# The head of a hybrid encoder block: GpSimd's first low parts behind VectorE's copies, and the first unit's products ordered by pass

## The chip, the cores and the metric

The kernel runs on one core of a Trainium2 chip. The metric is the device time of one execution in microseconds, lower is better. The core's engines are TensorE (PE; its weight loads are shown as PEld), VectorE (DVE), ScalarE (ACT), GpSimd (POOL) and SyncE (SP), which here only issues transfers.

## The reference

The block takes x (1 x 256 x 1024, float32) and computes

- h = RMSNorm(x), with a gain per channel, and z = h @ W_in, 8192 columns: pool input and gate, q, k, v of three groups of eight heads, attention gate, merge-gate logits;
- branch A: centred means over windows of 2, 4, 8 and 16 minus the token, a map per group, times SiLU of the gate, projected to 1024;
- branch B: attention in three groups with windows and strides (128,1), (512,4), (2048,16), each with a relative-position bias from a table of 32 buckets, merged by the softmax denominators, gated, projected to 1024;
- merge = sigmoid(gA) * yA + sigmoid(gB) * yB; x + merge @ W_out; a last RMSNorm.

All of it is float32. The changed part is the beginning: the first norm, its transposed output, and the first k columns of z:

```
def _rmsnorm(x, g):
    xf = x.astype(jnp.float32)
    r = lax.rsqrt(jnp.mean(xf * xf, axis=-1, keepdims=True) + RMS_EPS)
    return (xf * r).astype(x.dtype) * g
...
        h = _rmsnorm(x, norm_gain[l])
        z = h @ w_in[l]
```

## The kernel before, in words

**Split products.** Every float32 matrix product is made of three products of a rounded format (`F32R`). Each operand is cut into a high part, the value rounded to that format, and a low part, the rest: `whi` and `wlo` for weights, `hh` and `hl` for the normed activations. One 128x128 block of a product costs three matmuls (high by high, low by high, high by low), summed in PSUM (`mm3`, L253 to L256).

**Units of weights.** The weights stream in as units of 1 MB (a unit of W_in: 8 blocks of 128 rows, `kc` 0 to 7, by 256 columns; `load_next` issues one from SyncE, L101). Four raw buffers `wraw`, three pairs `whi`, `wlo`. Unit n is cut in halves of four `kc` by `cut_half` (L117): ScalarE writes `whi` (L128), VectorE subtracts and writes `wlo` (L133). TensorE uses each unit for two blocks of 128 columns, 24 matmuls each. The results leave PSUM through ScalarE and VectorE: three PSUM tiles of the tag `mm` take turns for them. Units 0, 1, 2 are the k columns of the three head groups; q and v follow, then the rest.

**Who sets the order.** In the head (L172 to L250) the order is written by hand: `tc.manual_schedule` keeps the order of the code for ScalarE, VectorE, TensorE and GpSimd. After it a scheduler orders the instructions of each engine from its own costs. SyncE's transfers stand in the order in which they are written. Each engine runs its instructions in order and waits on semaphores.

**The head.** Transfers go out in this order: x in two blocks of 128 rows, unit 0 in two halves, unit 1, the bias table `oh` (L147), unit 2, unit 3. ScalarE issues the parameters `prm` (L78), which hold among others the norm gain. Then:

1. TensorE runs twelve products of a zero tile (`keep_warm`, L179) that nothing reads.
2. For each of the two blocks of x, ScalarE and VectorE each square and sum one half (L185, L187), VectorE adds the two (L190), GpSimd raises the sum to -0.5 (L191). Then VectorE scales the first half of the columns (L194) and ScalarE the second (L195) into `XN`.
3. For unit 0 the cut is different: VectorE copies both halves of `wraw` to `whi` (L197) and GpSimd subtracts for `wlo` (L163), one half each after the copy of that half.
4. TensorE transposes the eight column blocks of the first block of x (L202), runs two products of the zero tile, transposes those of the second, runs one more. Four PSUM tiles `tp` take them, two column blocks each.
5. For each `kc`, ScalarE writes `hh` from PSUM times the gain (L228), and VectorE writes `hl` (L229), the rest. The fifth to eighth `hh` wait for the `hl` that reads the same PSUM tile.
6. TensorE multiplies unit 0 (`part0`, L207): for each `kc` two matmuls with `hh` (L212) and, right behind them, two with `hl` (L217); for the first four `kc` those with `wlo` follow after the sixth high one (L214), for the last four at the end. Then come three small products that look up the bias lines (L245); VectorE copies them out between the cuts of units 1 and 2 (L248).

After the head TensorE goes on with unit 1 at L254 to L256. GpSimd goes on with the masks and the transfers of the bias and the copies of k.

Of the kernel before, what the change touches and what calls it, by code (L numbers as in the profile page):

```python
# [17 lines left out]
P = 128  # L18
D = 1024
S = 256  # L20
KC = D // P
BW = 512
HD = 64
NH = 8
# [5 lines left out]
LROW = 9  # L30
LAG_T, LAG_O = 2, 2
RATES = 0.5, 0.667
WARM = 12, 2, 1
CUT = 640
POOL_W = (2, 4, 8, 16)
PAD = 8
# [6 lines left out]
def encoder_block(ctx: ExitStack, tc: tile.TileContext, x, w_in, lines, w_pool, w_proj_a, w_proj_b,  # L43
                  w_out, final_gain, params, out):
    nc = tc.nc
# [29 lines left out]


    prm = sb.tile([P, NPRM], F32, name="prm")
    nc.scalar.dma_start(prm, params)  # L78
    edge = prm[:, 28:28 + 8 * PAD].rearrange("p (g s e) -> p g s e", g=4, s=2)


# [61 lines left out]

    oh = slot([99, 3 * P + 2 * 3 * NH], F32, "uu", "oh")
    load_next()
    load_next()
    nc.sync.dma_start(oh, lines)  # L147
    load_next()


# [1 line left out]
    hh = sb.tile([P, KC, S], F32R, name="hh")  # L152
# [8 lines left out]
    def cut_lo(n, k0, k1, eng):  # L161
        t, (hi, lo) = raws[n][0], parts[n]
        return eng.tensor_tensor(lo[:, k0:k1, :], t[:, k0:k1, :], hi[:, k0:k1, :].bitcast(F32), op=ALU.subtract)  # L163
# [6 lines left out]
    with tc.manual_schedule(engines={mybir.EngineType.Activation, mybir.EngineType.DVE, mybir.EngineType.PE,  # L170
# [2 lines left out]
        warm = sb.tile([P, P], F32, name="warm")  # L173
        nc.vector.memset(warm, 0.0)
        nc.scalar.activation(tiny, warm[:, 0:1], AF.Square)

        def keep_warm(times):
            for _ in range(times):
# [16 lines left out]
            nc.scalar.activation(XN[:, b, halves[1]], X[:, b, halves[1]], AF.Copy, scale=rs[:, b:b + 1])  # L195
        for k in (0, 4):
            nc.vector.tensor_copy(parts[0][0][:, k:k + 4, :], raws[0][0][:, k:k + 4, :])  # L197
            first_lo = cut_lo(0, k, k + 4, nc.gpsimd)
        tps = [bank([P, 2, S], "mm" if i < 3 else "T", f"tp{i}", 3 if i < 3 else 2) for i in range(4)]

        def turn(kc, b):
# [2 lines left out]
        acc = bank([P, 2, 512], "S", "k00", 1)  # L204
        acc0 = [acc[:, u, 0:S] for u in range(2)]

        def part0(kc, lo):  # L207
            hi_, lo_ = parts[0]
            for u in range(2):
                c = slice(u * P, (u + 1) * P)  # L210
                if not lo:
                    nc.tensor.matmul(acc0[u], hi_[:, kc, c], hh[:, kc, :], start=kc == 0, stop=False)  # L212
                else:
                    nc.tensor.matmul(acc0[u], lo_[:, kc, c], hh[:, kc, :], start=False, stop=kc == KC - 1)  # L214
            for u in range(0 if lo else 2):
                c = slice(u * P, (u + 1) * P)
                nc.tensor.matmul(acc0[u], hi_[:, kc, c], hl[:, kc, :], start=False, stop=False)  # L217

        for kc in range(KC):
            turn(kc, 0)  # L220
        keep_warm(WARM[1])
        for kc in range(KC):
            turn(kc // 2 + kc % 2 * 4, 1)
        keep_warm(WARM[2])
        for kc in range(KC):
            v = tps[kc % 4][:, kc // 4].rearrange("p (j r) -> p r j", r=4)
            gcol = prm[:, kc:kc + 1]
            nc.scalar.activation(hh[:, kc, :].rearrange("p (r j) -> p r j", r=4), v, AF.Copy, scale=gcol)  # L228
            nc.vector.scalar_tensor_tensor(hl[:, kc, :].rearrange("p (r j) -> p r j", r=4), v, gcol,  # L229
                                           hh[:, kc, :].bitcast(F32).rearrange("p (r j) -> p r j", r=4),  # L230
                                           op0=ALU.mult, op1=ALU.subtract)
            if kc >= 2:
                part0(kc - 2, False)
            if kc == 5:
                for k in range(4):
                    part0(k, True)
        part0(6, False)
        part0(7, False)
        for kc in range(4, 8):
            part0(kc, True)  # L240

        for t in range(3):
            w = 3 * NH
            o = 3 * P + t // 2 * w
            nc.tensor.matmul(misc[:, t * w:(t + 1) * w], oh[:, t * P:(t + 1) * P], oh[:, o:o + w],  # L245
                             start=True, stop=True)
        cut_next()
        nc.vector.tensor_copy(line.rearrange("p i r h -> p r i h"),  # L248
                              misc[:, 0:LROW * NH].rearrange("p (r i h) -> p r i h", i=2, h=4))
# [566 lines left out]
```

## Time and profile before

Three runs: 267.93, 268.16 and 268.29 us; the median is 268.16.

| what | value |
| --- | --- |
| the profiled execution's own time | 268.12 us |
| its span, first to last instruction | 266.3 us |
| mean granted TensorE clock | 0.99 |
| busy PE, PEld | 254.3 us (95%), 250.4 us (94%) |
| busy DVE, ACT, POOL | 207.0 us (78%), 164.8 us (62%), 73.6 us (28%) |
| read from HBM | 47.42 MB, 182 GB/s over the span |

A row of the timeline reads: start, duration, engine, line, operation, output <- inputs, shapes, count, and in brackets the idle time of the engine before it and what ended that. Neighbouring instructions of one line are merged: `x8` are eight of them in the given time. A weight load (PEld) and its matmul (PE) are one product; an unrounded float32 product shows as two records of each. Times count from the start of the span.

### The profile page before, as it was taken

How to read it: one execution, taken by the hardware profiler on the slowest of the kernel's cores; microseconds unless marked ns; L12 is line 12 of the kernel's file. 1: busy time of each engine (PE TensorE's matmuls, PEld its weight loads, DVE VectorE, ACT ScalarE, POOL GpSimd, SP SyncE). 2: the span in 40 equal slices, each digit the busy share in tenths (PEclk: the TensorE clock that was granted, in tenths of full speed). 3: DMA queues.
4: the chain of work that ended last, by engine and by line, in shares of the span. 5: the costliest groups of instructions: out<-in, count | busy, mean ns of one | idle time of the engine just before them, and what ended most of it. 6: DMA issues, size and time to landing. Idle time of an engine off the chain costs nothing.

```text
span 266.3 us, 5321 instructions
## 1 busy us (share of the span) xinstructions
PE 254.3 (95%) x2088; PEld 250.4 (94%) x2088; DVE 207.0 (78%) x397; ACT 164.8 (62%) x283; POOL 73.6 (28%) x103
## 2 busy tenths in 40 slices
PE   7699999999999999999999999999999999999980
PEld 7599999999999999999999999999999999998870
DVE  2879877668888787889696986967859988899271
ACT  4596655667656565658956668655557797445141
POOL 1643293000799100010764910000010040442000
PEclk9999999999999999999999999999999999999996
DMA  6999999985444644444999966144440689300033
GB/s 231 396 411 303 213 327 305 304 308 188 159 160 158 236 161 160 159 160 158 270 260 235 286 229 244 41 160 158 160 158 0 207 321 280 145 4 0 0 79 79
DMA packets 9479, 51.99 MB, mean 195 GB/s; under 512 B 1147, under 2 KB 1374, under 8 KB 4206
## 3 DMA queue, kind: packets, MB, share of 16 engines
q1 hardware_dynamic: 6606, 43.95, 47.9%
q0 software_dynamic: 2544, 7.12, 12.0%
q10 hardware_dynamic: 304, 0.59, 0.6%
q8 instruction: 16, 0.26, 0.4%
q14 instruction: 9, 0.07, 0.1%
HBM read 47.42 MB, written 1.09 MB: 182 GB/s over the span
## 4 chain that ended last, share of the span: by engine, by line
PE 90%; issue 3%; DMA 3%; DVE 1%; ACT 1%; SPq 0%; POOLq 0%; POOL 0%
PE g L254 6%; PE g L255 6%; PE g L256 6%; PE q L255 4%; PE q L254 4%; PE q L256 4%; PE v L254 4%; PE v L255 4%; PE v L256 4%; PE k L254 4%; PE k L255 4%; PE k L256 3%; PE y L254 3%; PE y L255 3%; PE y L256 3%
## 5 line engine op out<-in xcount | busy, mean ns | idle before, releaser
L133 DVE TENSOR_TENSOR wlo<-wraw,whi 128x512 fp32r<-128x512 f32 (+2 forms) x134 | 105.2, 823 | 13.0 <-ACT whi L128 12.3
L128 ACT ACTIVATE whi<-wraw 128x1024 fp32r<-128x1024 f32 (+1 forms) x80 | 80.9, 1038 | 26.3 <-PE q L255 9.5
L254 PE MATMUL g<-hh,whi 128*128 128x256 f32 x128 | 36.2, 283 | 0.0
L255 PE MATMUL g<-hl,whi 128*128 128x256 f32 x128 | 35.7, 279 | 0.0
L256 PE MATMUL g<-hh,wlo 128*128 128x256 f32 x128 | 35.7, 279 | 0.0
L311 ACT ACTIVATE st<-st,nm 128x512 f32<-128x512 f32 x16 | 11.6, 723 | 28.8 <-DVE nm L308 28.8
L255 PE MATMUL q<-hl,whi 128*128 128x256 f32 x96 | 26.9, 280 | 0.0
L256 PE MATMUL q<-hh,wlo 128*128 128x256 f32 x96 | 26.8, 279 | 0.0
L254 PE MATMUL q<-hh,whi 128*128 128x256 f32 x96 | 26.8, 279 | 0.0
L254 PE MATMUL v<-whi,hh 128*128 128x256 f32 x96 | 26.6, 277 | 0.0
L255 PE MATMUL v<-wlo,hh 128*128 128x256 f32 x96 | 26.5, 276 | 0.0
L256 PE MATMUL v<-whi,hl 128*128 128x256 f32 x96 | 26.5, 276 | 0.0
L254 PEld LDWEIGHTS g<-hh,whi 128*128 128x128 f32 x128 | 24.1, 188 | 0.1
L255 PEld LDWEIGHTS g<-hl,whi 128*128 128x128 f32 x128 | 24.0, 188 | 0.0
L256 PEld LDWEIGHTS g<-hh,wlo 128*128 128x128 f32 x128 | 24.0, 188 | 0.0
L254 PE MATMUL k<-hh,whi 128*128 128x256 f32 x80 | 22.4, 280 | 0.0
L255 PE MATMUL k<-hl,whi 128*128 128x256 f32 x80 | 22.4, 280 | 0.0
L256 PE MATMUL k<-hh,wlo 128*128 128x256 f32 x80 | 22.3, 279 | 0.0
L254 PEld LDWEIGHTS q<-hh,whi 128*128 128x128 f32 x96 | 18.0, 188 | 0.0
L255 PEld LDWEIGHTS v<-wlo,hh 128*128 128x128 f32 x96 | 18.0, 188 | 0.0
L254 PEld LDWEIGHTS v<-whi,hh 128*128 128x128 f32 x96 | 18.0, 188 | 0.0
L255 PEld LDWEIGHTS q<-hl,whi 128*128 128x128 f32 x96 | 18.0, 188 | 0.0
(176 smaller groups left out, 735.7 us busy)
## 6 DMA issues: line engine op xcount, KB each, us to landing
wraw<-in_w_in_dram SPq DMA_DIRECT2D x31, 1024.0 KB, 6.3
wraw<-in_w_out_dram SPq DMA_DIRECT2D x4, 1024.0 KB, 6.1
T<-line_d POOLq DMA_DIRECT2D x4, 576.0 KB, 6.9
KX<-KX POOLq DMA_DIRECT2D x8, 256.0 KB, 14.3
wraw<-in_w_proj_a_dram SPq DMA_DIRECT2D x2, 1024.0 KB, 4.8
wraw<-in_w_proj_b_dram SPq DMA_DIRECT2D x2, 1024.0 KB, 4.7
X<-in_x_dram SPq DMA_DIRECT2D x2, 512.0 KB, 4.2
wraw<-in_w_in_dram SPq DMA_DIRECT2D x2, 512.0 KB, 6.5
```

What stands on the lines that cost most here:

```text
L128: nc.scalar.activation(hi[:, s, :], t[:, s, :], AF.Copy)
L133: nc.vector.tensor_tensor(lo[:, s, :], t[:, s, :], hi[:, s, :].bitcast(F32), op=ALU.subtract)
L254: nc.tensor.matmul(acc, ah, bh, start=first, stop=False)
L255: nc.tensor.matmul(acc, ah, bl, start=False, stop=False)
L256: nc.tensor.matmul(acc, al, bh, start=False, stop=last)
L311: e = nc.scalar.activation(st, st, AF.Exp, bias=nm, scale=-1.0, accum_out=l)
```

## The change

- GpSimd's two subtractions of unit 0 stand behind both copies of VectorE, and are cut 5 and 3 `kc` instead of 4 and 4. The first one reads from both halves, so it waits for the second copy.
- The products of unit 0 go by pass: with `hh` as each `kc` comes, with `hl` two `kc` behind, and all those with `wlo` at the end.
- The products of the zero tile are 17 at the beginning instead of 12, none between the two blocks' transposes instead of two, and two after them instead of one.
- The three lookups of the bias lines stand after the first product with `hl`, instead of at the end.
- The transfer of `oh` goes ahead of unit 1's instead of behind it.
- ScalarE issues the parameters after its first activation instead of at once.

The diff:

```
-WARM = 12, 2, 1
+WARM = 17, 2
...
     prm = sb.tile([P, NPRM], F32, name="prm")
-    nc.scalar.dma_start(prm, params)
...
     oh = slot([99, 3 * P + 2 * 3 * NH], F32, "uu", "oh")
     load_next()
+    nc.sync.dma_start(oh, lines)
     load_next()
-    nc.sync.dma_start(oh, lines)
     load_next()
...
         nc.scalar.activation(tiny, warm[:, 0:1], AF.Square)
+        nc.scalar.dma_start(prm, params)
...
         for k in (0, 4):
             nc.vector.tensor_copy(parts[0][0][:, k:k + 4, :], raws[0][0][:, k:k + 4, :])
-            first_lo = cut_lo(0, k, k + 4, nc.gpsimd)
+
+        cut_lo(0, 0, 5, nc.gpsimd)
+        first_lo = cut_lo(0, 5, 8, nc.gpsimd)
...
-        def part0(kc, lo):
+        def part0(kc, x):
             hi_, lo_ = parts[0]
             for u in range(2):
                 c = slice(u * P, (u + 1) * P)
-                if not lo:
-                    nc.tensor.matmul(acc0[u], hi_[:, kc, c], hh[:, kc, :], start=kc == 0, stop=False)
-                else:
-                    nc.tensor.matmul(acc0[u], lo_[:, kc, c], hh[:, kc, :], start=False, stop=kc == KC - 1)
-            for u in range(0 if lo else 2):
-                c = slice(u * P, (u + 1) * P)
-                nc.tensor.matmul(acc0[u], hi_[:, kc, c], hl[:, kc, :], start=False, stop=False)
+                nc.tensor.matmul(acc0[u], (lo_ if x == 2 else hi_)[:, kc, c], (hl if x == 1 else hh)[:, kc, :],
+                                 start=x == 0 and kc == 0, stop=x == 2 and kc == KC - 1)
 
         for kc in range(KC):
             turn(kc, 0)
-        keep_warm(WARM[1])
         for kc in range(KC):
             turn(kc // 2 + kc % 2 * 4, 1)
-        keep_warm(WARM[2])
+        keep_warm(WARM[1])
...
+            part0(kc, 0)
             if kc >= 2:
-                part0(kc - 2, False)
-            if kc == 5:
-                for k in range(4):
-                    part0(k, True)
-        part0(6, False)
-        part0(7, False)
-        for kc in range(4, 8):
-            part0(kc, True)
-
-        for t in range(3):
-            w = 3 * NH
-            o = 3 * P + t // 2 * w
-            nc.tensor.matmul(misc[:, t * w:(t + 1) * w], oh[:, t * P:(t + 1) * P], oh[:, o:o + w],
-                             start=True, stop=True)
+                part0(kc - 2, 1)
+            if kc == 2:
+
+                for t in range(3):
+                    w = 3 * NH
+                    o = 3 * P + t // 2 * w
+                    nc.tensor.matmul(misc[:, t * w:(t + 1) * w], oh[:, t * P:(t + 1) * P], oh[:, o:o + w],
+                                     start=True, stop=True)
+        for kc in (6, 7):
+            part0(kc, 1)
+        for kc in range(KC):
+            part0(kc, 2)
```

Three places show what this does to the engines' instructions. The first is TensorE from the transposes of the second block (`tp`) to the first products of unit 0, whose sum is the tile `k`. Before:

```order
L179 MATMUL misc<-warm 128x128 x2
L202 MATMUL tp_135<-ident,XN 128x128 [waits DVE_49]
L202 MATMUL tp_135<-ident,XN 128x128 [waits Activation_49]
L202 MATMUL tp_136<-ident,XN 128x128 x2
L202 MATMUL tp_137<-ident,XN 128x128 x2
L202 MATMUL tp_138<-ident,XN 128x128 x2
L179 MATMUL misc<-warm 128x128
L212 MATMUL k_139<-hh,whi_125 128x256 [waits DVE_49,Activation_49]
L212 MATMUL k_139<-hh,whi_125 128x256
L217 MATMUL k_139<-hl,whi_125 128x256 [waits DVE_49]
```

And now:

```order
L204 MATMUL tp_140<-ident,XN 128x128 [waits Activation_49]
L204 MATMUL tp_141<-ident,XN 128x128 x2
L204 MATMUL tp_142<-ident,XN 128x128 x2
L204 MATMUL tp_143<-ident,XN 128x128 x2
L179 MATMUL misc<-warm 128x128 x2
L213 MATMUL k_144<-hh,whi_130 128x256 [waits DVE_49,Activation_49]
L213 MATMUL k_144<-hh,whi_130 128x256
L213 MATMUL k_144<-hh,whi_130 128x256 [waits Activation_49]
L213 MATMUL k_144<-hh,whi_130 128x256
L213 MATMUL k_144<-hh,whi_130 128x256 [waits Activation_49]
L213 MATMUL k_144<-hh,whi_130 128x256
L213 MATMUL k_144<-hl,whi_130 128x256 [waits DVE_49]
```

Three pairs with `hh` now stand ahead of the first wait for `hl`, where one stood; the bias lines follow the first pair with `hl`, and the sixteen products with `wlo` are the last.

The second place is GpSimd between the two powers of the norm and the masks of the bias. Before:

```order
L191 TENSOR_TENSOR rs<-rt_115,mhalf 128x1 [waits DVE_49,Pool_49]
L191 TENSOR_TENSOR rs<-rt_122,mhalf 128x1 [waits DVE_49]
L163 TENSOR_TENSOR wlo_126<-wraw_76,whi_125 128x1024 [waits DMAHW3_49,DVE_49]
L163 TENSOR_TENSOR wlo_126<-wraw_76,whi_125 128x1024 [waits DMAHW4_49,DVE_49]
L485 MEMSET BT_600 64x4x64 x2
```

And now:

```order
L191 TENSOR_TENSOR rs<-rt_120,mhalf 128x1 [waits DVE_49,Pool_49]
L191 TENSOR_TENSOR rs<-rt_127,mhalf 128x1 [waits DVE_49]
L162 TENSOR_TENSOR wlo_131<-wraw_75,whi_130 128x1280 [waits DMAHW4_49,DMAHW3_49,DVE_49]
L162 TENSOR_TENSOR wlo_131<-wraw_75,whi_130 128x768
L480 MEMSET BT_604 64x4x64 x2
```

The first subtraction waits for both halves of unit 0 and for VectorE's second copy; the second waits for nothing more. VectorE's own instructions stand in the same order as before.

The third place is SyncE's first transfers, where `wraw_76`, `wraw_79` and `wraw_82` are units 0, 1 and 2. Before:

```order
L70 DMA X<-in_x_dram 128x1024 x2
L110 DMA wraw_76<-in_w_in_dram 128x1024 x2
L112 DMA wraw_79<-in_w_in_dram 128x2048
L147 DMA oh<-in_lines_dram 99x432
L112 DMA wraw_82<-in_w_in_dram 128x2048
```

And now, where the units are `wraw_75`, `wraw_79` and `wraw_81`:

```order
L70 DMA X<-in_x_dram 128x1024 x2
L109 DMA wraw_75<-in_w_in_dram 128x1024 x2
L145 DMA oh<-in_lines_dram 99x432
L111 DMA wraw_79<-in_w_in_dram 128x2048
L111 DMA wraw_81<-in_w_in_dram 128x2048
```

The bias table has changed places with unit 1. After the head the scheduler puts ScalarE's second half cut of unit 3 behind some copies of k instead of ahead of them; the other engines' order there is the same.

## The prediction

> **What bounds the kernel now.** I read four views in this order: the stretches of the span, the waits of TensorE, the first 19 us in order of time, and the transfers.
>
> Stretches (microseconds; busy time and instructions of PE, PEld, DVE, ACT, POOL; granted clock; DMA share; GB/s), ahead of them the page's first line and its row of DMA use in 40 slices:
>
> ```profile
> span 266.3 us, 5321 instructions
> DMA  6999999985444644444999966144440689300033
> ...
> 0.00:12.17 12.17, 7.78 (x48) 7.38 (x48) 6.50 (x13) 5.86 (x13) 4.72 (x11) 1.00 0.82 305
> 12.17:205.00 192.83, 192.83 (x1659) 192.83 (x1660) 155.87 (x304) 126.86 (x223) 57.20 (x78) 1.00 0.67 212
> 205.00:256.00 51.00, 51.00 (x362) 47.71 (x361) 40.69 (x73) 29.53 (x42) 11.12 (x14) 1.00 0.38 125
> ```
>
> From 12.17 to 256 us TensorE never pauses: 192.83 busy of 192.83, then 51.00 of 51.00, at the full granted clock. All its idle time lies in the head and in the last 10 us. So a microsecond that TensorE starts earlier at the end of the head is a microsecond off the end, as long as data keeps up. The longest of TensorE's waits says what held the head (who waited for whom, microseconds in total, times, longest):
>
> ```profile
> PE k L217 <- DVE hl L229: 2.0, 1, 2.0
> ```
>
> They are the wait for the first `hl`. The head in order of time (start, duration, engine, line) shows why it was late:
>
> ```profile
> 1.05 4.91 PE L179 MATMUL misc<-warm 128*128 128x128 f32 x24 [1.05 <-DVE warm L174]
> 7.26 1.09 PE L202 MATMUL tp<-ident,XN 128*128 128x128 f32 x8 [1.30 <-DVE XN L194]
> 7.65 0.72 ACT L195 ACTIVATE XN<-X,rs 128x512 f32<-128x512 f32 x1 [0.47 <-POOL rs L191]
> 8.05 0.69 DVE L197 CAST whi<-wraw 128x1024 fp32r<-128x1024 f32 x1
> 8.19 0.61 PE L179 MATMUL misc<-warm 128*128 128x128 f32 x4
> 8.82 2.35 POOL L163 TENSOR_TENSOR wlo<-wraw,whi 128x1024 fp32r<-128x1024 f32 x1 [1.20 <-DVE whi L197]
> 9.04 2.68 DVE L197 CAST whi<-wraw 128x1024 fp32r<-128x1024 f32 x1 [0.31 <-DMA wraw<-in_w_in_dram]
> 9.06 1.57 ACT L228 ACTIVATE hh<-tp,prm 128x256 fp32r<-128x256 f32 x4 [0.69 <-PE tp L202]
> 9.65 0.49 PE L212 MATMUL k<-hh,whi 128*128 128x256 f32 x2
> 11.64 3.22 DVE L229 SCALAR_TENSOR_TENSOR hl<-tp,prm,hh 128x256 fp32r<-128x256 f32 x8
> 11.80 2.40 POOL L163 TENSOR_TENSOR wlo<-wraw,whi 128x1024 fp32r<-128x1024 f32 x1 [0.63 <-DVE whi L197]
> 12.17 0.50 PE L217 MATMUL k<-hl,whi 128*128 128x256 f32 x2 [2.03 <-DVE hl L229]
> 13.70 3.89 ACT L128 ACTIVATE whi<-wraw 128x1024 fp32r<-128x1024 f32 x4
> 14.78 2.36 DVE L133 TENSOR_TENSOR wlo<-wraw,whi 128x1024 fp32r<-128x1024 f32 x2
> 18.28 0.36 PE L254 MATMUL k<-hh,whi 128*128 128x256 f32 x1
> 18.48 0.23 DVE L248 COPY line<-misc 128x72 f32<-128x72 f32 x1 [1.34 <-PE misc L245]
> ```
>
> The two copies of L197 have one shape. The first took 0.69 us; the second began at 9.04, took 2.68 and ended at 11.72, which is 0.55 us after GpSimd's subtraction (8.82 + 2.35 = 11.17). So GpSimd, already running, held the copy up, and `hl`, next on VectorE, began at 11.64 instead of about 9.7. The eight `hl` (0.40 us apart) ran beside GpSimd's second subtraction without loss: that form is not held up.
>
> **The change part by part.**
>
> *GpSimd behind both copies.* The second copy then takes what the first took: 9.04 + 0.69 = 9.73. `hl` runs from 9.73 to 12.95 (3.22). GpSimd starts 0.08 later, as it did after the first copy (8.74 to 8.82), at 9.81; at 2.35 us per 1024 elements its 1280 end at 12.75 and its 768 at 14.51.
>
> *Transposes unheld, warm-up moved.* The second block needs ScalarE's half of `XN`, done at 7.65 + 0.72 = 8.37, and I let TensorE follow 0.08 later, like GpSimd behind the copy. Eight transposes in 1.09 us with 0.27 for the last are 0.117 apart, so from 8.45 seven of them end their slots at 9.27; the first `hh` starts near 8.8 instead of 9.06. Two warm-up products (four records, 0.112 apart: (0.61 - 0.27) / 3) follow. The first real product issues at about 9.75, 0.1 later than the 9.65 of before. I take no gain from that. The five added warm-up products at the beginning are ten records: 1.05 + 4.91 + 10 x 0.112 = 7.08, before the transposes could start at 7.26, so they cost nothing. If they ran at the early pace (4.91 / 24 = 0.20), they would end at 8.0 and the start would move to about 10.35; if X comes 0.2 sooner it may be 9.5. These are the bounds.
>
> *Products by pass.* Nothing is added: 48 products and three bias lines before and after. Their price is in the chain of waits:
>
> ```profile
> 16.91 0.94 PE k L214 x8
> 17.86 0.58 PE misc L245 x6
> ```
>
> A product takes 0.94 / 8 = 0.1175, the bias lines 0.58. Check on before: 46 products from 12.17 are 5.41, with 0.58 that is 18.16; the next weights began at 18.28, so 0.12 is left for the handover. After: 9.75 + 48 x 0.1175 + 0.58 + 0.12 = 16.09, if no operand is late. The operands: the first `hl` (0.47, which is 3.22 less seven steps of 0.393) is done at 10.20 and wanted after three pairs, at 10.46; the last at 12.95, wanted at 13.86. GpSimd's first piece is done at 12.75 and wanted at 9.75 + 32 x 0.1175 + 0.58 = 14.09; its second at 14.51, wanted ten products later, at 15.27. The bias lines are wanted at 10.9, and their transfer now stands ahead of the second weights instead of behind them.
>
> So TensorE's next weights begin 18.28 - 16.09 = **2.19 us earlier**. What must keep up with that:
>
> *The second unit's low parts* move to where GpSimd's second piece runs. Both read two operands from SBUF, and later in the same trace such a pair meets:
>
> ```profile
> 129.65 1.29 POOL L554 TENSOR_TENSOR SA<-SA,sgsa 128x512 f32<-128x512 f32 x1
> 132.20 2.38 DVE L133 TENSOR_TENSOR wlo<-wraw,whi 128x1024 fp32r<-128x1024 f32 x1
> 133.42 2.31 POOL L554 TENSOR_TENSOR SB<-SB,sgsb 128x512 f32<-128x512 f32 x1
> 137.76 1.23 DVE L133 TENSOR_TENSOR wlo<-wraw,whi 128x1024 fp32r<-128x1024 f32 x1
> ```
>
> Alone they take 1.29 and 1.23 us, there 2.31 and 2.38: each waits out a whole instruction of the other. The Trainium skill's page "SBUF — State Buffer", section "Who interferes with whom", states just that for VectorE with two SBUF inputs against a GpSimd instruction that reads SBUF: whichever issues first holds the shared ports and the other blocks fully. If the two did not block each other, the first low half, ready to start at 13.2 (below), would be done at 14.4.
>
> I take the blocked case. VectorE's half waits for 14.51 and is done at 15.7, the next at 16.9 (1.18 each). TensorE wants them at 16.09 + 2 x 0.1175 = 16.33 and 16.09 + 14 x 0.1175 = 17.74. They hold with 0.6 and 0.8 us.
>
> *VectorE further on.* It reaches the line copy at 16.9 instead of 18.48, only 1.58 ahead of before, since it no longer waits 1.34 there. TensorE is 2.19 ahead, so every slack between them shrinks by 0.6. The tightest I find is the reuse of the three product banks: this low part ends at 28.10, and TensorE takes its bank back with the third unit, at 18.28 + 96 x 0.1175 = 29.56:
>
> ```profile
> 27.22 0.88 DVE L435 TENSOR_TENSOR KX<-k,KX 64x256 fp32r<-64x256 f32 x2
> ```
>
> 1.46 us become 0.8. No wait.
>
> *Transfers.* The second weights were issued at 2.60 and landed 9.1 later, at 11.7; the 167.1 KB of bias lines now go ahead, at about 410 GB/s 0.4 us, so 12.1. ScalarE is free for them at about 11.95 (its last `hh` follows the fourth `hl`, 9.73 + 3 x 0.393 + 0.47 = 11.4, and takes about 0.5), so this delays its cut by 0.15: the first half is cut 12.1 + 1.05 (one of the four cuts of 3.89 at 13.70) = 13.15 on, which lies under GpSimd's hold. The DMA engines are full until about 60 us (the page's 9s), so the later weights are a question of their own. For the eighth unit: issue and landing, and ScalarE's use of it:
>
> ```profile
> wraw<-in_w_in_dram SPq DMA_DIRECT2D x1, 1024.0 KB, 9.1
> 2.60 0.53 SPq L112 DMA_DIRECT2D wraw<-in_w_in_dram  x1
> oh<-in_lines_dram SPq DMA_DIRECT2D x1, 167.1 KB
> 26.12 0.33 SPq L112 DMA_DIRECT2D wraw<-in_w_in_dram  x1
> wraw<-in_w_in_dram SPq DMA_DIRECT2D x1, 1024.0 KB, 12.4
> 41.06 1.06 ACT L128 ACTIVATE whi<-wraw 128x1024 fp32r<-128x1024 f32 x1 [1.87 <-PE q L255]
> ```
>
> Landed at 38.5, used at 41.06: 2.5 us, more than 2.19 even if the landing stays where it is, and TensorE itself uses that unit some 10 us after the cut. No cost.
>
> *The parameters* are now issued after ScalarE's table load and first activation instead of ahead of them:
>
> ```profile
> 0.74 0.41 ACTq L78 DMA_DIRECT2D prm<-in_params_dram  x1
> 1.18 1.28 ACT L175 ACT_TABLE_LOAD   x1 [1.18 <-PEq L803]
> 2.48 0.20 ACT L175 ACTIVATE tiny<-warm 128x1 f32<-128x1 f32 x1
> prm<-in_params_dram ACTq DMA_DIRECT2D x1, 64.0 KB, 4.0
> K<-K POOLq DMA_DIRECT2D x2, 256.0 KB, 14.6
> ```
>
> With the table load first, the issue falls at about 2.3, and with 4.0 us they land at 6.3; `hh` wants them at 8.8. Upper bound from the nearest crowded rows, the K copies: 14.6.
>
> **Sum.** 268.12 us is this execution's own time (span 266.3, the rest around it), and the median is 268.16. 268.12 - 2.19 = **265.9**.
>
> **The rivals.**
>
> 1. *The ports go the other way.* If GpSimd's first piece ends after VectorE's first low half is ready (13.2), VectorE takes the ports and GpSimd's second piece starts at 14.4, ends at 16.2, and TensorE, which wants it at 15.27, stalls 0.9. That gives 266.8; a late start (10.35) gives 266.5. Against it: GpSimd's pieces follow each other at 12.75, 0.45 before.
> 2. *The change does not free the copy.* If something else held it (it began 0.3 late on its own transfer), `hl` is ready at 12.2 as before. Six `hh` products are done by then; the other 42 give 12.2 + 4.94 + 0.58 + 0.12 = 17.8, a gain of 0.4: 267.7. For it: only one such copy is on view. Against: its end follows GpSimd's by just an uncontended remainder.
> 3. *The gain is given back downstream*, through the full DMA engines or VectorE's shorter lead: 268.1. Against it the slacks above; for it, that the tenth unit's transfer shows no landing in the trace.
> 4. *Slower: the parameters come late.* They then share the engines with the activations and the first weights. It decides once they land after about 11.3: `hh` to first product is 0.59 (9.06 to 9.65), and 11.35 + 0.59 + 5.64 + 0.58 + 0.12 is the 18.28 of before. At the K copies' 14.6 us they land at 16.9, and TensorE ends the head at 23.8, 5.6 later than before: 273.7. Against it, before, their 64 KB took 4.0 us while X moved. The Trainium skill's "DMA: Bandwidth & Descriptors", section "Queues, rings and completion order", says each engine takes turns between its queues packet by packet, which speaks against it too.
>
> **How the numbers follow.** The forecast has 0.70, rival 1 0.12, rival 2 0.06, rival 3 0.07, rival 4 0.05. The forecast's own spread comes from the start (9.5 to 10.35): 265.5 to 266.6. The range takes in rival 1 and a little below for X coming sooner: **265.4 to 267.2**. A measurement here tells about 0.2% (0.54 us) from no change. Faster: the forecast and rival 1, 0.82. Same: rivals 2 and 3, 0.13. Slower: 0.05.
>
> **What would show it.** Second copy 0.7 us instead of 2.68; `hl` from about 9.7; no wait of TensorE for `hl` above 0.2; the first low half of the second unit stretched to the end of GpSimd's second piece; the next weights at about 16.1; TensorE without pause after that. It would be wrong if the copy still ends behind GpSimd, if `hh` starts after 9.3, if TensorE waits for GpSimd's low parts, or if waits of TensorE appear between 18 and 60 us.

## The result, and the profile after

Over twelve executions each the changed kernel has a median of 267.29 us (265.56 to 269.49), the kernel before, beside it on the same chip, 269.01 (267.89 to 270.04). The ratio is 0.9937, with an interval of 0.9909 to 0.9965: 0.6% or 1.7 us faster. The forecast was 265.9, its range ended at 267.2. So the sign was right, and the gain was smaller than forecast.

One thing must be known to read these times: in some executions TensorE's clock is halved for about 3.4 us in the head, which costs 1.6 us. The times of each kernel fall into two groups by that. Of the kernel before, 50 of the 97 executions of this study lie in the upper group (269.31 to 270.20); the others (267.52 to 268.55) have a median of 268.16, and the three runs shown are of these. Of the changed kernel, 4 of 24 lie in the upper group. With the full clock on both sides it is 268.16 against about 267.15: **1.0 us, where 2.2 were forecast.** The rest of the 1.7 is the clock.

The profiled execution of the changed kernel took 268.98 us. It is one of the four, and must be read with that in mind. The longest of TensorE's waits (who waited for whom, microseconds in total, times, longest), in the kernel after:

```profile
PE misc L179 <- DVE warm L173: 1.1, 1, 1.1
PE k L213 <- DVE hl L225: 1.0, 1, 1.0
PE k L213 <- ACT hh L224: 0.2, 1, 0.2
```

The wait for `hl` went from 2.0 to 1.0, not to nothing. Rows of the head of the kernel after, in order of time (start, duration, engine, line), show why:

```profile
0.73 1.28 ACT L174 ACT_TABLE_LOAD   x1 [0.73 <-PEq L798]
1.04 0.42 ACTq L175 DMA_DIRECT2D prm<-in_params_dram  x1
1.05 6.45 PE L179 MATMUL misc<-warm 128*128 128x128 f32 x34 [1.05 <-DVE warm L173]
8.63 1.57 ACT L224 ACTIVATE hh<-tp,prm 128x256 fp32r<-128x256 f32 x4 [0.59 <-PE tp L204]
9.00 0.69 DVE L197 CAST whi<-wraw 128x1024 fp32r<-128x1024 f32 x1 [1.20 <-DMA wraw<-in_w_in_dram]
9.85 0.94 PE L213 MATMUL k<-hh,whi 128*128 128x256 f32 x6 [0.15 <-ACT hh L224]
10.65 0.69 DVE L197 CAST whi<-wraw 128x1024 fp32r<-128x1024 f32 x1 [0.95 <-DMA wraw<-in_w_in_dram]
11.26 3.22 DVE L225 SCALAR_TENSOR_TENSOR hl<-tp,prm,hh 128x256 fp32r<-128x256 f32 x8
11.43 4.73 POOL L162 TENSOR_TENSOR wlo<-wraw,whi 128x1280 fp32r<-128x1280 f32 x2 [4.15 <-DVE whi L197]
19.05 0.28 PE L249 MATMUL k<-hh,whi 128*128 128x256 f32 x1
```

The second copy takes 0.69 us instead of 2.68, as forecast. But it begins at 10.65 instead of 9.04, since VectorE waits 0.95 for the transfer: the second half of unit 0 landed 1.6 us later than in the trace of before. `hl` began at 11.26, only 0.38 sooner than the 11.64 of before.

The next weights began at 19.05, later than before's 18.28. The stretches (microseconds; busy time and instructions of PE, PEld, DVE, ACT, POOL; granted clock; DMA share; GB/s) hold the other part:

```profile
10.00:13.00 3.00, 1.99 (x16) 1.79 (x16) 2.35 (x6) 1.42 (x5) 1.57 (x1) 0.99 1.00 388
13.00:16.00 3.00, 3.00 (x16) 3.00 (x16) 2.46 (x5) 2.43 (x4) 3.00 (x2) 0.50 1.01 418
18.50:40.00 21.50, 21.50 (x185) 21.50 (x184) 18.13 (x27) 15.11 (x26) 10.73 (x15) 1.00 1.02 318
```

From 13 to 16 us the granted clock is 0.50, and 16 products stand where the full clock fits 28 (such a stretch stands below). The half clock lasts some 3.4 us (12.9 to 16.3) and costs half of them, 1.7. Without it the next weights would begin near 17.35, 1.25 after the 16.09 of the forecast. From 18.5 us to the last 10 us TensorE never pauses again.

### The profile page after: what moved, and what is told of

It is laid out like the page before. It is cut to its first block, busy times and chain, and to the rows that moved or that the text cites. A ratio compares the mean times of both kernels' runs of the same rounds, so it can differ in the third digit from the quotient of the medians.

```text
span 267.2 us, 5336 instructions
## 1 busy us (share of the span) xinstructions
PE 257.4 (96%) x2096; PEld 253.5 (95%) x2096; DVE 206.9 (77%) x397; ACT 165.2 (62%) x283; POOL 74.0 (28%) x103
## 4 chain that ended last, share of the span: by engine, by line
PE 91%; DMA 3%; issue 2%; DVE 1%; ACT 1%; SPq 0%; POOLq 0%; POOL 0%
PE g L249 6%; PE g L250 6%; PE g L251 6%; PE q L249 4%; PE q L250 4%; PE q L251 4%; PE v L250 4%; PE v L249 4%; PE v L251 4%; PE k L249 4%; PE k L250 4%; PE k L251 3%; DMA wraw<-in_w_in_dram 3%; PE y L249 3%; PE y L250 3%; PE y L251 3%
## 5 line engine op out<-in xcount | busy, mean ns | idle before, releaser
L132 DVE TENSOR_TENSOR wlo<-wraw,whi 128x512 fp32r<-128x512 f32 (+2 forms) x134 | 107.0, 837 | 13.5 <-ACT whi L127 12.7
L251 PEld LDWEIGHTS v<-whi,hl 128*128 128x128 f32 x96 | 18.0, 188 | 0.0
```

What stands on the lines that cost most here:

```text
L132: nc.vector.tensor_tensor(lo[:, s, :], t[:, s, :], hi[:, s, :].bitcast(F32), op=ALU.subtract)
L251: nc.tensor.matmul(acc, al, bh, start=False, stop=last)
```

## The experiments

No kernel here leaves out any of the computation. All ratios are against the kernel before, run beside it on the same chip; they mix its two groups of times. The first four experiments ran on one chip, the next four on another, the last four on a third. At the full clock the kernel before had medians of 268.15, 267.98 and 268.20 us there, so times of different chips compare to about 0.2.

### The kernel before, once more

No edit.

> The kernel before, unchanged, for a second trace of it and for the clock of each of its runs. Its twelve times so far lie in two groups, 267.9 to 268.3 and 269.7 to 270.0 us. Theory A (the landing): unit 0's second half lands at another time in each execution, 9.0 us in the one trace of before and 10.6 us in the one of after, but before does not feel it as long as it lands ahead of GpSimd's release of the ports at 11.2 us. Then the lower group stays within 0.3 us whatever the landing. Theory B (the clock): the upper group are executions in which TensorE's granted clock falls to 0.5 for 3.4 us in the head, as in the trace of after (12.9 to 16.3 us), which costs 1.7 us of work. Then the runs near 269.8 show a mean clock about 0.006 lower (3.4 x 0.5 / 268) than those near 268.0. If neither holds, the clock is the same in both groups.

Median 269.51, ratio 1.0007 (0.9984 to 1.0031). Four executions lie at 268.02 to 268.43, eight at 269.37 to 269.80. The profiled one is of the upper group. Its timeline:

```profile
8.99 2.78 DVE L197 CAST whi<-wraw 128x1024 fp32r<-128x1024 f32 x1 [0.21 <-DMA wraw<-in_w_in_dram]
...
19.84 0.36 PE L254 MATMUL k<-hh,whi 128*128 128x256 f32 x1
```

One of its stretches, columns as above:

```profile
13.00:16.00 3.00, 3.00 (x16) 3.00 (x15) 3.00 (x7) 3.00 (x6) 2.29 (x5) 0.50 1.00 415
```

The copy is held as in the first trace. What sets the upper group apart is the clock of 0.50 behind the wait for `hl`; the next weights begin at 19.84 instead of 18.28, 1.56 later, and the execution is 1.58 longer. The kernel's two groups are this, and nothing else that the trace shows. Where an execution's mean clock is known, it is 0.983 to 0.989 in the upper group and 0.987 to 0.996 in the lower.

### GpSimd behind both copies, and nothing else

In the kernel before:

```
         for k in (0, 4):
             nc.vector.tensor_copy(parts[0][0][:, k:k + 4, :], raws[0][0][:, k:k + 4, :])
+        for k in (0, 4):
             first_lo = cut_lo(0, k, k + 4, nc.gpsimd)
```

> The kernel before with one part of the change: GpSimd's two subtractions of unit 0 stand behind both of VectorE's copies, still four blocks each. My prediction's step: the second copy takes 0.7 us instead of 2.68. Theory A: it then ends 0.7 us after unit 0's second half lands, 9.7 to 11.4 us, hl follows, and the runs spread over up to 2 us below 268.0 where those of before lay within 0.4. The products with the low parts come earlier in this order than in the changed kernel (behind the sixth hh), wanted about 2.1 us after the first hl; GpSimd's first piece is done 2.45 us after the copy and so at most 0.2 us late: gain 0.5 to 2.0 us, time 266.0 to 267.5 in the undisturbed runs. Rival: the hold on the copy was no loss since something else sets the start, then 268.0.

268.09 us, ratio 0.9983 (0.9958 to 1.0008). The timeline of its profiled execution (269.88 us, one of the upper group):

```profile
8.84 2.36 POOL L163 TENSOR_TENSOR wlo<-wraw,whi 128x1024 fp32r<-128x1024 f32 x1 [1.20 <-DVE whi L197]
9.19 2.56 DVE L197 CAST whi<-wraw 128x1024 fp32r<-128x1024 f32 x1 [0.43 <-DMA wraw<-in_w_in_dram]
```

The edit was empty. GpSimd still starts at 8.84, when the first copy is done: moving the lines of one engine past those of another changes neither engine's order nor what it waits for. In the change it is the cut of five and three `kc` that makes GpSimd wait, since its first piece reads from both halves. So this kernel did not test the copy by itself; the kernels below that have the cut do.

### The bias lines' transfer back behind unit 1, the lookups left early

In the kernel after:

```
     load_next()
-    nc.sync.dma_start(oh, lines)
     load_next()
+    nc.sync.dma_start(oh, lines)
     load_next()
```

> The changed kernel with the bias table's transfer put back behind unit 1. If the table, whose 1.7 KB packets moved at 8 to 10 us beside unit 0's last packets, is what made unit 0's second half land at 10.6 instead of 9.0 us, then it lands near 9.0 again, and the undisturbed runs gather near 266.0 us. If the landing varies by itself, the runs spread as those of the changed kernel did (265.6 to 267.9). Where the lookups of the bias lines then wait for the table on TensorE, in front of most products, it is slower instead: the table landed at about 11.9 us in before, against 10.9 us wanted, which costs about 1 us.

271.37 us (269.52 to 272.13), ratio 1.0082 (1.0052 to 1.0111), slower than before. The wait, in TensorE's waits of this kernel:

```profile
PE misc L236 <- DMA oh<-in_lines_dram: 2.2, 1, 2.2
```

The lookups stand in the middle of TensorE's order, and everything behind them waits for the table. So the early lookups need the early transfer: the two edits belong together, and an experiment that wants the old transfers must put the lookups back to the end too. The second copy began at 9.71 here, later than the 8.99 to 9.19 of the kernel before with its own transfers. The wait is not all: eight of the nine executions have mean clocks of 0.979 to 0.989, and only the fastest, 269.52, has 0.995. The profiled one ran from 13.7 to 20.5 us at half clock.

### Seven products of the zero tile in the gap of the kernel before

```
+            if kc == 0 and not lo:
+                keep_warm(7)
```

> The kernel before with seven more products of the zero tile (14 records, about 1.6 us) between the first products with hh and the first with hl, where TensorE stood idle for 2.0 us. They end before the first hl is there, so by the instructions alone the time stays 268.0 us. Theory B: TensorE's idle time in the head is what brings the half clock; filled, the group near 269.8 us thins out or is gone, and the mean clock is the higher one in all runs. Theory A alone: both groups remain as before.

Median 268.27, eleven of twelve executions within 267.89 to 268.59, one at 269.29; ratio 0.9978 (0.9957 to 0.9998). The timeline of this kernel:

```profile
9.94 1.72 PE L179 MATMUL misc<-warm 128*128 128x128 f32 x14
12.15 0.51 PE L219 MATMUL k<-hl,whi 128*128 128x256 f32 x2 [0.49 <-DVE hl L231]
```

And its stretch behind the wait:

```profile
13.00:16.00 3.00, 3.00 (x28) 3.00 (x27) 3.00 (x7) 3.00 (x5) 2.26 (x5) 1.00 1.01 418
```

Work that nobody reads fills 1.72 of the 2.0 us that TensorE stood idle, `hl` comes no sooner, and the upper group is down to one in twelve. So this idle time is what brings the half clock; with 0.49 us of it left, and the 1.3 us that TensorE waits ahead of the transposes as before, the half clock is rare. With the clock even, this kernel takes 268.27 against the 268.16 of before: the seven products are free.

### The two transfer edits, one at a time

The parameters issued first again, in the kernel after:

```
     prm = sb.tile([P, NPRM], F32, name="prm")
+    nc.scalar.dma_start(prm, params)
...
         nc.scalar.activation(tiny, warm[:, 0:1], AF.Square)
-        nc.scalar.dma_start(prm, params)
```

> The changed kernel with the parameters' issue put back ahead of ScalarE's table load; the bias table stays ahead of unit 1. In four traces with the transfers of before, X landed at 4.5 to 4.6 and 5.8 to 5.9 us and unit 0's halves at 7.8 to 7.95 and 8.9 to 9.15; in two with the later parameters X came at 4.0 to 4.2 and 5.5 to 5.7, and unit 0's halves at 8.5 to 9.0 and 9.7 to 10.6. Theory T (the transfers' order delays unit 0; both edits share in it): X back at 4.5 and 5.9, the second half at 9.2 to 9.8, undisturbed runs 266.0 to 266.9. If the table alone is to blame, the second half stays at 10.0 or later; if the parameters alone, it is at 9.0 and the runs gather at 266.0. Rival V (the landing varies by itself): spread as in the changed kernel, 265.6 to 267.9.

The bias table behind unit 1 again with its lookups at the end, the parameters left late:

```
     load_next()
-    nc.sync.dma_start(oh, lines)
     load_next()
+    nc.sync.dma_start(oh, lines)
     load_next()
...
-            if kc == 2:
-                for t in range(3):
...
         for kc in range(KC):
             part0(kc, 2)
+        for t in range(3):
...
```

> The changed kernel with the bias table's transfer behind unit 1 and the lookups at the end of the head, both as before, so that TensorE does not wait for the table; the parameters stay late. Theory T: the second half of unit 0 lands at about 9.7, as in the run with the table put back alone (which lost 2.2 us waiting for the table), hl starts at 10.3, and the undisturbed runs gather at 266.2 to 267.0. If the parameters have no share, 9.0 and 266.0. Rival V: spread over 2 us.

Both edits at once, so that the transfers go as in the kernel before and only the order of the products, the warm-up and GpSimd's cut are new:

> The changed kernel without its edits on transfers: parameters first, table behind unit 1, lookups at the end. Everything else of the change stays. My prediction's sum was made on these landings: second half of unit 0 at 9.0, copy done at 9.7, first weights of unit 1 at 16.1 to 16.3, 265.9 us, and with theory T the undisturbed runs gather within 0.5 us of it, below the changed kernel's median of 267.3. GpSimd's second piece is wanted 0.58 us sooner than with the lookups in between (14.7 against 14.5 done), so up to 0.2 us may be lost there. Rival V: the same spread and median as the changed kernel's (265.6 to 267.9).

| the kernel after with | us, lowest to highest | ratio | second copy begins | next weights begin |
| --- | --- | --- | --- | --- |
| both transfers as before | 266.0 (265.86 to 266.18, 4 runs) | 0.9884 (0.9852 to 0.9915) | 9.17 | 16.18 |
| the parameters first | 265.83 (265.54 to 266.18, 4 runs) | 0.9877 (0.9845 to 0.9910) | 9.41 | 16.28 |
| the table behind unit 1 | 266.31 (265.89 to 267.09, 6 runs) | 0.9895 (0.9865 to 0.9926) | 9.39 | 16.41 |
| neither: as it is, this study's second series | 267.18 (266.57 to 270.74, 12 runs) | 0.9940 (0.9915 to 0.9965) | 9.80 | 16.67 |

The first row comes near the forecast: 266.0 us against 265.9, next weights at 16.18 against 16.09. Against the full-clock median beside it, 267.98, it gains 2.0 of the 2.2 us. Its timeline:

```profile
9.17 0.69 DVE L197 CAST whi<-wraw 128x1024 fp32r<-128x1024 f32 x1 [0.43 <-DMA wraw<-in_w_in_dram]
9.78 3.22 DVE L225 SCALAR_TENSOR_TENSOR hl<-tp,prm,hh 128x256 fp32r<-128x256 f32 x8
9.94 4.80 POOL L163 TENSOR_TENSOR wlo<-wraw,whi 128x1280 fp32r<-128x1280 f32 x2 [2.32 <-DVE whi L197]
12.93 4.03 DVE L133 TENSOR_TENSOR wlo<-wraw,whi 128x1024 fp32r<-128x1024 f32 x2
14.80 0.76 PEld L213 LDWEIGHTS k<-hh,wlo 128*128 128x128 f32 x6 [0.18 <-POOL wlo L163]
16.18 0.36 PE L247 MATMUL k<-hh,whi 128*128 128x256 f32 x1
```

So the order of the products, GpSimd's cut and the warm-up gain nearly what the sum said, and **the gain that is missing lies in the two transfer edits.** Neither of them alone costs it: with either one undone the time is within 0.3 us of the first row. Together they cost about 1.0: 267.18 is 1.2 above 266.0, but the last row ran on another chip, and against the full-clock medians beside them the two kernels gain 1.0 and 2.0.

Part of that is arithmetic. By the forecast's own row the first `hl` was done 0.26 us before it was wanted, so in the forecast's order copies up to about 9.3 cost nothing. With the parameters first the copy begins 0.24 later than in the first row and the next weights only 0.10.

In the first and third row another path decides. With the lookups at the end, TensorE wants GpSimd's second piece 0.58 us sooner, and in the first row the loading of its weights waits 0.18 for it (14.80 above). GpSimd is done at 14.74 there (9.94 + 4.80) and the next weights begin 1.44 later; with the table behind unit 1 it is done at 14.95 and they begin 1.46 later. On that path a later copy has no slack. In that third row the products also begin later, at 9.98 instead of 9.62, so the wait for GpSimd adds only about 0.1.

How the two delays join is not settled. Twice 0.2 would put the second copy at 9.6. The two traces of the changed kernel show 9.80 and 10.65, and the kernel before with both edits 9.48 (next experiment). The table behind unit 1 has a second trace, that of the kernel which waited for the table: 9.71 with the same transfers as the 9.39 of the third row. So the landing moves by some tenths between executions too.

### The new transfers in the kernel before

```
-    nc.scalar.dma_start(prm, params)
...
     load_next()
-    load_next()
     nc.sync.dma_start(oh, lines)
     load_next()
+    load_next()
...
         nc.scalar.activation(tiny, warm[:, 0:1], AF.Square)
+        nc.scalar.dma_start(prm, params)
```

> The kernel before with the change's transfers alone (parameters late, table ahead of unit 1). Theory T: unit 0's halves land at 8.5 to 9.0 and 9.7 to 10.6 as in the changed kernel. In before GpSimd's first piece starts behind the first copy, which now starts up to 1.0 us later (8.5 to 9.0 instead of 8.05), so the hold on the second copy ends as much later and the undisturbed runs are up to 1.0 us slower than 268.1: 268.3 to 269.1. If the landing is no matter of order, 268.1 and halves at 7.9 and 9.0.

Median 268.43 (seven executions at 267.80 to 268.53, five at 269.39 to 272.19), ratio 0.9996 (0.9967 to 1.0024): no difference. Its second copy:

```profile
9.48 2.18 DVE L197 CAST whi<-wraw 128x1024 fp32r<-128x1024 f32 x1 [0.81 <-DMA wraw<-in_w_in_dram]
```

It begins 0.44 later than in the trace of before and ends at 11.66, as before (11.72): the copy waits for GpSimd, and its landing can move by as much as the hold lasts without anyone noticing. In the kernel before the transfers' order costs nothing that these runs show, in the changed one it does.

### One late landing of known size, in both

The bias table's transfer between the two halves of unit 0, once in the kernel with the old transfers and the new order, once in the kernel before:

```
                 k = shp[0] // 2
+                if h:
+                    nc.sync.dma_start(oh, lines)
                 nc.sync.dma_start(t[:, h * k:(h + 1) * k, :], src[:, h * k:(h + 1) * k, :])
...
-    nc.sync.dma_start(oh, lines)
```

> The changed kernel with the transfers of before (parameters first, lookups at the end, 266.0 us), but with the bias table between the two halves of unit 0, so that the second half lands later: 167 KB, 0.4 to 0.9 us, 9.6 to 10.1 instead of 9.2. Theory: with the hold gone the time follows the landing, so 0.2 to 0.9 us slower, 266.2 to 266.9. If the landing does not matter, 266.0.

> The kernel before with the same delay: the bias table between the two halves of unit 0. Theory: GpSimd holds the second copy to 11.2 us anyway, so a landing at 9.6 to 10.1 changes nothing: the lower group stays at 267.7 to 268.5 (upper near 269.7), and the second copy ends at 11.7 as before. If the landing sets the copy's end in before too, 0.4 to 0.9 us slower.

With the new order, the timeline:

```profile
9.95 0.70 DVE L198 CAST whi<-wraw 128x1024 fp32r<-128x1024 f32 x1 [1.32 <-DMA wraw<-in_w_in_dram]
16.95 0.36 PE L248 MATMUL k<-hh,whi 128*128 128x256 f32 x1
```

and TensorE's waits:

```profile
PE k L214 <- DVE hl L226: 0.5, 1, 0.5
```

In the kernel before, the timeline:

```profile
10.09 1.61 DVE L198 CAST whi<-wraw 128x1024 fp32r<-128x1024 f32 x1 [1.38 <-DMA wraw<-in_w_in_dram]
```

With the new order the landing is 0.78 later than with the old transfers, the next weights come 0.77 later (16.95 against 16.18), and the time goes from 266.0 to 266.98 (266.64 to 267.14; ratio 0.9931, 0.9905 to 0.9958). Against the full-clock medians beside the two kernels, 267.98 and 268.20, the loss is 0.76 instead of 0.98. In the kernel before the landing is 1.05 later than in its first trace, the copy ends at 11.70, and the time stays: 268.29, ratio 0.9998 (0.9971 to 1.0025). This is the clearest pair of the study. The same delay is hidden under the hold before the change and stands on the path after it. Here too the path runs through GpSimd: its second piece ends at 15.49 and the next weights begin 1.46 later. So the kernel comes within 0.2 us of the changed kernel's time with one late copy, though not on quite the same path.

### The changed kernel, once more

No edit.

> The changed kernel, unchanged, for a second trace of it beside the others. Theory T, now: the parameters' late issue together with the table ahead of unit 1 makes unit 0's second half land late and by another amount in each execution (9.7 to 10.6 us), the changed kernel's time follows it one for one from 9.2 on, and the runs spread over about 2 us above 265.6; with the parameters first the same kernel gave 265.5 to 266.2. Expected here: median 266.5 to 267.5, first weights of unit 1 in the trace at 16.1 us plus the landing's excess over 9.2 (plus 1.7 if the clock halves). Rival: the tight runs of the kernels with the parameters first were luck of that chip; then this one is as tight there, 265.5 to 266.2.

Ten executions lie at 266.57 to 267.44, two at 269.19 and 270.74; median 267.18. The profiled one took 267.32 at the full clock. Its timeline:

```profile
9.80 0.69 DVE L197 CAST whi<-wraw 128x1024 fp32r<-128x1024 f32 x1 [0.89 <-DMA wraw<-in_w_in_dram]
16.67 0.28 PE L249 MATMUL k<-hh,whi 128*128 128x256 f32 x1
```

and TensorE's waits:

```profile
PE k L213 <- DVE hl L225: 0.7, 1, 0.7
```

The next weights begin 0.58 after the forecast's 16.09. This execution is 1.4 above the forecast, so the other 0.8 arose behind the head, where TensorE has no pause. From the next weights to the end of the span it takes 265.5 - 16.67 = 248.8 us, while the other traces take 247.6 to 248.5 (before: 266.3 - 18.28 = 248.0; the first trace of the change: 267.2 - 19.05 = 248.1). That is 0.3 more than the longest of the others. It is one trace of two, and what it is due to stays open (last section).

### The lookups as filler

In the kernel with the parameters first, no products of the zero tile behind the transposes, and the three lookups ahead of the first product with `hl` instead of behind it:

```
-WARM = 17, 2
+WARM = 17, 0
...
             part0(kc, 0)
-            if kc >= 2:
-                part0(kc - 2, 1)
             if kc == 2:
...
+            if kc >= 2:
+                part0(kc - 2, 1)
```

> For a faster version: the changed kernel with the parameters issued first, without the two products of the zero tile behind the transposes, and with the lookups of the bias lines ahead of the first product with hl instead of behind it. The first product with hh can then start at 9.4 instead of 9.85 us, the lookups (0.58 us) fill the wait for the first hl (10.6), and TensorE ends the head at 9.4 + 6.34 = 15.75 instead of 16.3: up to 0.5 us below the 265.8 of the kernel with the parameters first, 265.3 to 265.8. GpSimd's second piece (15.0 done, 14.9 wanted) and unit 1's first low half (16.15 done, 16.0 wanted) then stand close and may take 0.2 back. If the table lands after 10.1 the lookups wait and the gain is gone.

265.76 us (265.18 to 266.24), ratio 0.9889 (0.9856 to 0.9922). The next weights begin at 15.81, 0.47 earlier than with the parameters first alone, but the times of the two kernels overlap (265.83): whether that is a gain isn't told apart here. Both are faster than the kernel before and than the change as it was made.

## Why the prediction was right or wrong

**The bound** was right: what TensorE gains at the end of the head is a gain at the end. The late half of known size costs 0.77 us at the next weights and 0.76 at the end (0.98 as the medians stand), and in no trace does TensorE pause between the head and the last 10 us.

**The copy** was right: 0.69 or 0.70 us instead of 2.68 in every kernel in which GpSimd waits for both halves. Rival 2 is out.

**Transposes and warm-up.** The first `hh` began at 8.63 (forecast about 8.8) and the first product at 9.85 (9.75). But the early products of the zero tile did not cost nothing in that trace: they ended at 7.50 instead of 7.08, and the transposes, whose input was ready at 6.87 since X had come 0.5 sooner, began behind them at 7.34. That TensorE then waited 1.0 for `hl` made it harmless. In the eight traces of the new order the 34 records took 5.84 to 6.98 us, where the forecast had 6.03.

**The price of the passes** was right to 0.2 us, and its near hit partly luck. 48 products, three bias lines and the handover were to end at 16.09 and ended at 16.18, in the kernel whose copy began at 9.17. But there the products began at 9.62, 0.13 before the forecast, and waited 0.18 for GpSimd, which the order of the forecast, with the lookups in between, would not have done. In the forecast's own steps the bias lines were wanted at 10.69 (9.75 and eight products), not at 10.9; nothing hung on that.

**The ports.** The second unit's two low halves took 4.03 us from 12.93 where they take 2.36 alone, and ended at 16.96; the forecast had 16.9. The Trainium skill's "SBUF — State Buffer", section "Who interferes with whom", has VectorE with two SBUF inputs wait out a GpSimd instruction that reads SBUF, and this trace agrees. GpSimd kept the ports, so rival 1 is out, but by luck: the forecast saw GpSimd's first piece end 0.45 us before VectorE's low half was ready. The two pieces in this kernel (durations in ns, least, median and longest, then first and last start):

```profile
L163 POOL TENSOR_TENSOR wlo<-wraw,whi x2: 1852/2417/2982, 9.9 to 12.9; 128x1280 fp32r<-128x1280 f32 x1, 128x768 fp32r<-128x768 f32 x1
```

The first ended at 12.92 (9.94 + 2.98), and the low half began at 12.93. In the second trace of the change it is 13.52 against 13.56. TensorE did not wait for GpSimd in the changed kernel; with the lookups at the end it did, for 0.18. Of rival 3 no wait appeared between the head and 60 us.

**The step that failed is the term "second copy 9.04".** It was read from one trace of before as if it were a property of the transfers. There the copy ended at 11.72 and needs 0.69 by itself, so the hold hid any landing up to about 11.0. One profile could not show how far the landing moves, and the last two edits of the change both moved it. `hl`, forecast to start at 9.73 and to keep TensorE waiting 0.2 at most, started at 11.26 and 10.41 in the two traces, and TensorE waited 1.0 and 0.7 for it. The working priced the two transfer edits only by what they themselves carry: the bias table by 0.15 us of unit 1, the parameters by whether `hh` would wait. The parameters themselves were in time, so rival 4 is out. The row of DMA issues of the kernel after (KB, us from issue to landing):

```profile
prm<-in_params_dram ACTq DMA_DIRECT2D x1, 64.0 KB, 3.1
```

Issued at 1.04, they landed at 4.1. What came late was another transfer. The landings as the starts of the second copy show them: 8.99 to 9.41 in the seven traces with the parameters first and the halves together (9.20 and 9.41 in the two of them with the table ahead of unit 1), 9.39 to 10.65 in the five with the parameters late.

A second error sits beside it and did no harm by itself: the parameters were to be issued at about 2.3, behind the table load. They were issued at 1.04, during it.

**What no step held** is the clock. The three times shown were all of one group, and the forecast took 268.1 for the kernel before as a whole. The run beside the changed kernel gave 269.01. That flatters the ratio: a kernel with less idle time in its head also meets the half clock less often.

The sum, put right for the second trace of the change: 265.9, plus about 0.6 for the landing, plus 0.8 behind the head, which makes 267.3 against the 267.32 of that execution. For the first trace: 265.9, plus about 1.25 for the landing (copy at 10.65), plus 1.7 for the clock, which makes 268.85 against 268.98. That a late landing costs this is shown, by undoing either transfer edit and by the late half. The 0.8 has been seen in one trace, without its cause, so how much of the missing 1.2 is the landing in a usual execution stays open: half of it in one trace, all of it in the other.

## What to carry to other kernels

Before a hold is removed, look at what else it hides: an operand that lands anywhere under it has no visible slack, and one trace's landing is no bound for the next. Price a moved transfer by the transfers that it overtakes or meets, not only by whether it is itself in time; and try the order of the transfers and the order of the work as separate edits, since here the work alone gave 2.0 of the 2.2 us. A kernel that comes in two groups of times should be forecast for each group.

## What the runs showed of the hardware

**An idle head can cost clock.** Idle gaps of TensorE of 2.0 us in the kernel before, and of 1.0 us in the changed kernel's first trace, at 10 to 12 us, were followed by some 3.4 us at a granted clock of 0.50; by their times, 50 of 97 and 4 of 24 executions had that. Behind the wait of 2.2 us for the table it was twice as long, 13.7 to 20.5 us. With 0.5 us left idle it was 1 of 12, and in the 27 executions of the five kernels that had the new order with waits for `hl` of 0.5 us at most it did not appear once. The Trainium skill's "TensorE: Matmul & The Clock Gate", section "Part 1: The HAM clock gate", tells of a free-running window of about 3.4 us, after an idle one of which the clock is halved. The two values of the clock and the length of the stretches, once and twice 3.4 us, agree with that, and a free-running window would explain why the same kernel meets it in one execution and not in the next. But the section's rule of thumb, no idle gaps over about 3.4 us, is too lenient here: 2.0 us sufficed, and once 1.0.

**Products have two paces at the full clock.** In the same stretch, without a pause, the records count 215 products in one execution and 223 in another. The kernel with the old transfers and the changed kernel's second trace:

```profile
17.00:42.00 25.00, 25.00 (x223) 25.00 (x223) 22.34 (x33) 18.74 (x32) 11.21 (x15) 1.00 1.02 322
```

```profile
17.00:42.00 25.00, 25.00 (x215) 25.00 (x214) 22.16 (x32) 17.52 (x30) 13.40 (x17) 1.00 1.03 327
42.00:62.00 20.00, 20.00 (x172) 20.00 (x171) 14.20 (x25) 10.89 (x19) 0.00 (x0) 1.00 0.89 258
```

That is 0.112 against 0.116 us a product. Records missing from a trace would not explain it: both traces, like the others of the new order with all products of the zero tile, hold 2096. Without a pause and at an even clock only the pace can lengthen what follows the head. The other traces count either 180 or 181 products from 21 to 42 us and then 176 to 178 from 42 to 62, or 187 or 188 and then 173 or 174; the changed kernel's second one has 181 and then 172, the slower count in both. From 21 to 62 us together it counts 350 products, all other traces 354 to 359, and four products are 0.5 us. What sets the pace isn't known.

**A transfer's issue on ScalarE's queue does not wait for its table load**: it began at 1.04 us, the load ran from 0.73 to 2.01, and so, to 0.01 us, in all five traces with the parameters late.

**Small transfers can move a large one's landing by more than their size: seen once.** In the first trace of the change the same bytes were asked for as before, 64 KB of them 0.3 us later and 167 KB ahead of unit 1, and the second half of unit 0 landed 1.6 us later. From 9 to 11 us the engines were as busy as before and moved less, first in the kernel before, then after:

```profile
9.00:11.00 2.00, 1.14 (x11) 0.93 (x8) 1.96 (x1) 1.57 (x4) 2.00 (x1) 1.00 0.96 403
```

```profile
9.00:11.00 2.00, 1.64 (x13) 1.27 (x11) 1.04 (x2) 1.20 (x4) 0.00 (x0) 1.00 0.97 304
```

403 GB/s became 304 at the same share. In the other two traces with both transfer edits the landing was 0.4 and 0.8 us later, and 393 and 385 GB/s moved; the 231 KB at 403 GB/s are 0.6 us. So clearly more than their size is seen in one trace only, and which transfer's packets took the time isn't known.
